# RWKV-7 scan of a diffusion trunk: each chunk as one affine map of the state, and triangular inverses begun on GpSimd with 16x16 blocks

## The chip, the cores and the metric

The kernel runs on one core of one Trainium2 chip. The metric is the time of one execution on the device in microseconds (us). A core has TensorE (PE in the profile, its weight loads PEld), VectorE (DVE), ScalarE (ACT), GpSimd (POOL) and SyncE (SP), which here only issues DMAs.

## The reference, cut to what matters

The program is a trunk of two layers over 512 latent tokens and 256 context tokens of width 1024. A layer is half a SwiGLU, a token mixer, and half a SwiGLU. The mixer of layer 0 is HGRN2, that of layer 1 is a bidirectional RWKV-7; the change lies in the scan of the latter. For each of 16 heads (64 wide) and each direction it computes, token by token,

```python
def step(s, inp):                       # s: 64 x 64 state of a head
    dec, kt, vt, kkt, bt = inp[:5]
    sa = jnp.einsum('bhvk,bhk->bhv', s, kkt)
    s = s * dec[:, :, None, :] - sa[..., None] * bt[:, :, None, :] + vt[..., None] * kt[:, :, None, :]
    y = jnp.einsum('bhvk,bhk->bhv', s, inp[5]) if with_out else None
    return s, y
```

first over the 256 context tokens, from a zero state and without outputs, then from that state over the 512 latent tokens.

## The kernel before

`rwkv_scan` works in chunks of 64 tokens. Within a chunk the 64 rank-one corrections depend on one another through a strictly triangular 64x64 matrix N, so a chunk needs the inverse of (I - N). With it the chunk is a few 64x64 products.

The work is cut into twelve items `(qd, g)`: `qd` is a group of four heads (0 to 3), `g` is 0 for the context and 1 or 2 for the two halves of the latent tokens. An item has two directions `d`, two head pairs `e`, two heads `hp` of a pair (on partitions 0 to 63 and 64 to 127) and four chunks `c`: 32 chunks of one head and direction. Five generators make an item:

- `prep_a` (line 1225) loads the features, forms the decays (`sw`, `cum`) and the scaled keys (`KR`, `BK`), multiplies them (`A`, line 1304), masks the products to N and Ar, and writes the 32x32 diagonal blocks of N to DRAM (`md`, line 1318) by eight DMAs on SP, one block to a partition: 64 blocks.
- `prep_m` (line 1323) is GpSimd's: it loads the blocks to 64 partitions (`M<-md`, line 1330), inverts each by 30 steps of two instructions (a product into `mt`, line 1336, an addition into `M`, line 1337) on up to 240 elements of a partition, and stores them (`me<-M`, line 1340).
- `prep_d` (line 1344) loads the inverted blocks into `P1` by eight DMAs on SP (`P<-me`).
- `prep_b` (line 1352) loads the values (`VU`), turns `BK` (`bkt`), and forms `W`, the part of the correction that the values alone give.
- `prep_c` (line 1386) transposes the blocks on VectorE (`PT`, line 1391) and forms the off-diagonal 32x32 blocks by 64 products of 32x32 (`TT`, line 1409, `Yo`, line 1411), copied into the inverse by four instructions.

`scan` (line 1430) then goes through four chunk steps one after another, for both directions and pairs at once, with the state in `G`. A step is four groups of products with work on other engines between them: `kG` (16 products), `rhs` = kG + W on VectorE, `U` = inverse times rhs (16), two copies of U into `VU` on ScalarE, `G` (16), two VectorE instructions that add the old state and scale it, and for latent items `y` (32 products, four of one kind and four of the other in turn) with two copies. `readout` normalizes a finished `qd`.

The main loop at line 1555 takes the items in order. While `scan` of item k yields, it advances the inversions (`RM` steps at each yield), the preparation of later items (`RP`: two steps of `prep_a` of k+2, then `prep_d` of k+1, the rest of `prep_a` of k+2, `prep_b` and `prep_c` of k+1), and the readout (`RO`). The tile framework takes this order and priorities (`urgent`), simulates a timeline, and fixes one order of instructions for each engine; on the chip every engine keeps its order and waits on semaphores. Buffers come in rings: `Q` of 13 and 15 tiles (`NQ1`, `NQ2`), PSUM banks of tag "a" (two, for `prep_a`), "b" (two, for `prep_b`, `prep_c` and the readout), "s" (four, for the scan).

Before the loop the value projection (`value_steps`) runs on PE beside the preparation and inversion of item 0. After it come the output projection and the last SwiGLU.

Of the kernel before, what the change touches and what calls it, by code (L numbers as in the profile page):

```python
# [9 lines left out]
F32 = mybir.dt.float32  # L10
# [16 lines left out]
NQ1, NQ2 = 13, 15  # L27
RM, RP, RO, RV, RF = 3.0, 5.0, 0.3, 1.5, 1.3
# [40 lines left out]
NCST = 790  # L69
# [4 lines left out]
def trunk(ctx, tc, io, phases=None, dump=None):  # L74
# [1105 lines left out]

    def rwkv_scan(l):
# [5 lines left out]
        masks = [cst2[:, 260 + 128 * d:388 + 128 * d] for d in range(2)]  # L1187
        PP = open_psum("PP")
# [3 lines left out]
        def Q(name):  # L1192
            first = "B2" not in late or name in Q1
            return (B1 if first else late["B2"]).tile([128, 1024], F32, tag="Q", name=name, bufs=NQ1 if first else NQ2)
# [18 lines left out]
        diagonal = [[B1.tile([128, 16, 64], F32, name=f"P1_{i}{d}") for d in range(2)] for i in range(2)]  # L1213
        for d in range(2):
            dve.memset(diagonal[0][d], 0.0)
            pool.memset(diagonal[1][d], 0.0)
        FE, ME = dve, pool
        slot = lambda hp, e, c: hp * 8 + e * 4 + c
# [3 lines left out]
        lanes = [(d, hp, b, d * 32 + (hp * 2 + b) * 8, 64 * hp + 32 * b) for d in range(2) for hp in range(2) for b in range(2)]  # L1222
        ready, inverse = {}, {}

        def prep_a(qd, g):
# [9 lines left out]
            gs = B1.tile([128, 4], F32, tag="gs", name="gs", bufs=3)  # L1235
# [84 lines left out]
            ready[qd, g] = KR, BK, N, Ar, gt, gs, md  # L1320
            yield

        def prep_m(qd, g):
# [4 lines left out]
            me = dram.tile([64, 32, 32], F32, tag="me", name="me", bufs=2)  # L1328
            M = Q("M")[0:64, :1024].rearrange("l (s t) -> l s t", t=32)
            pool.dma_start(out=M, in_=md)  # L1330
            eng = ME
            mt = B1.tile([64, 256], F32, tag="mt", name="mt", bufs=2)
            for j in range(30, 0, -1):
                n = 31 - j
                t = mt[:, :j * n].rearrange("l (a b) -> l a b", b=n)
                eng.tensor_tensor(t, M[:, 0:j, j:j + 1].to_broadcast([64, j, n]), M[:, j:j + 1, j + 1:32].to_broadcast([64, j, n]), ALU.mult)  # L1336
                eng.tensor_tensor(M[:, 0:j, j + 1:32], M[:, 0:j, j + 1:32], t, ALU.add)  # L1337
                yield
            eng.memset(M.rearrange("l s t -> l (s t)")[:, 0:1024:33], 1.0)
# [4 lines left out]
        def prep_d(qd, g):  # L1344
            while (qd, g) not in inverse:
                yield
            me = inverse[qd, g]
            P1 = inverse[qd, g] = diagonal[(3 * qd + g) % 2]
            for d, hp, b, l0, r0 in lanes:
                nc.sync.dma_start(out=P1[d][r0:r0 + 32, 8 * hp:8 * hp + 8, 32 * b:32 * b + 32], in_=me[l0:l0 + 8].rearrange("l s t -> s l t"))  # L1350

        def prep_b(qd, g):
            KR, BK, N, Ar, gt, gs, _ = ready[qd, g]
# [17 lines left out]
            W = Q("W").rearrange("p (i n) -> p i n", i=4)  # L1371
            for i2 in range(2):
                p = bank("W")
                for i in range(2):
                    for d in range(2):
                        c = chunk(d, 2 * i2 + i)
                        for e in range(2):
                            for hp in range(2):
                                o = 256 * i + 64 * (2 * d + e)
                                pe.matmul(p[half(hp), o:o + 64], N[d][half(1 - hp), slot(hp, e, c)],  # L1380
                                          VU[half(1 - hp), d, c, hp, e], start=True, stop=True)
                act.activation(W[:, 2 * i2:2 * i2 + 2], p.rearrange("p (i n) -> p i n", i=2), AF.Copy)
                yield
            ready[qd, g] = KR, N, Ar, BKT, VU, W, gt, gs

        def prep_c(qd, g):
            KR, N, Ar, BKT, VU, W, gt, gs = ready[qd, g]
            P1 = inverse.pop((qd, g))
            PT = [late["B2"].tile([128, 16, 32], F32, tag="PT0", name="PT0", bufs=1), Q("PT").rearrange("p (s n) -> p s n", n=64)]
            for d in range(2):  # L1390
                dve.transpose(PT[d], P1[d][:, :, :32 + 32 * d])
                yield
            Y = [P1[0], PT[1]]
# [3 lines left out]
            for stage in range(2):  # L1397
                for e in range(2):
                    for c in range(4):
                        for d in range(2):  # L1400
                            for hp in range(2):
                                s = slot(hp, e, c)
                                lo = 32 * (s % 8)
                                a = 64 * hp + 32 * d
                                b = 64 * hp + 32 * (1 - d)
                                ca, cb_ = 32 * d, 32 * (1 - d)
                                if stage == 0:
                                    other = (PT[0] if d == 0 else P1[1])[a:a + 32, s, ca:ca + 32]
                                    pe.matmul(pt[b:b + 32, lo:lo + 32], N[d][a:a + 32, s, cb_:cb_ + 32], other, start=True, stop=True, tile_position=(a, b))
                                else:  # L1410
                                    pe.matmul(py[a:a + 32, lo:lo + 32], tt[b:b + 32, lo:lo + 32], Y[d][b:b + 32, s, cb_:cb_ + 32], start=True, stop=True, tile_position=(b, a))
                    yield
                if stage == 0:
                    act.activation(tt, pt[:, :256], AF.Copy)
            for d in range(2):
                for hp in range(2):
                    a = 64 * hp + 32 * d
                    src = py[a:a + 32, :256].rearrange("p (s n) -> p s n", n=32)
                    dst = Y[d][a:a + 32, 8 * hp:8 * hp + 8, 32 * (1 - d):32 * (1 - d) + 32]
# [4 lines left out]
            ready[qd, g] = (KR, Ar, BKT, VU, Y, W, gt, gs)  # L1424
# [5 lines left out]
        def scan(qd, g, KR, Ar, BKT, VU, Y, W, gt, gs):  # L1430
# [4 lines left out]
            Gt = lambda: late["B2"].tile([128, 4, 64], F32, tag="G", name="G", bufs=3)  # L1435
            G = None
            if lat:
                G = Gt()
                dve.tensor_tensor(G, state["G"], gs.unsqueeze(2).to_broadcast([128, 4, 64]), ALU.mult)
            for i in range(4):  # L1440
                cs = (i, 3 - i)
                at = lambda d, e: slice(64 * (2 * d + e), 64 * (2 * d + e) + 64)
                if G is not None:
                    p = bank("kG", "s")
                    for d, e in DE:
                        for hp in range(2):
                            pe.matmul(p[half(hp), at(d, e)], KR[d][half(hp), 4 * e + cs[d], 0], G[half(hp), 2 * d + e], start=True, stop=True)
                    rhs = late["B2"].tile([128, 256], F32, tag="rhs", name="rhs", bufs=2)
                    dve.tensor_tensor(rhs, p[:, :256], W[:, i], ALU.add)
# [312 lines left out]
```

## Time and profile before

| | us |
|---|---|
| median of 3 runs | 3897.82 |
| lowest and highest of them | 3892.38 and 3904.64 |
| the profiled execution | 3901.05 |
| its span, first to last instruction | 3899.3 |
| mean granted TensorE clock, share of full | 0.926 |

An execution's time is its span plus about 2 us. The page of the profile gives for each engine the sum of the times of its instructions; matmuls are pipelined, so that the time of one is longer than the distance to the next. [...]

### The profile page before, as it was taken

The numbers are of one execution on the slowest core, as the hardware profiler recorded it, in microseconds if no ns is written. First come the engines' busy times: TensorE is split into PE (matmuls) and PEld (weight loads), VectorE is DVE, ScalarE is ACT, GpSimd is POOL, SyncE is SP. The second block draws the span as 40 slices with busy tenths as digits, with TensorE's granted clock in tenths as the row PEclk, the third lists the DMA queues.
The fourth block names the chain that finished last, engine by engine and source line by source line (L and its number), as shares of the span: only waits on it lengthen the run. The fifth ranks groups of instructions, "written<-read, shape, count | busy, mean of one in ns | idle before, by whom it ended". The sixth has DMA issues, their size and how long they took to land. (4 is left out here: it accounts for less than half of the span.)

```text
span 3899.3 us, 61645 instructions
## 1 busy us (share of the span) xinstructions
PE 3551.6 (91%) x24898; PEld 3115.9 (80%) x24898; DVE 2529.3 (65%) x4042; ACT 1310.4 (34%) x2024; POOL 1382.0 (35%) x1395
## 2 busy tenths in 40 slices
PE   5999998899999899999899999698978889889998
PEld 3898997688888688888799998576867777668887
DVE  6766667656666866666766675776444554468886
ACT  4332333232322432333532333354322222244343
POOL 4212213433433422122422221522366766523332
PEclk9999999999999899999999999798967776779999
DMA  5332331411112233333132332247633332233332
GB/s 186 115 96 88 97 98 44 114 43 44 39 44 66 66 113 103 103 110 113 52 95 82 90 95 78 66 155 240 164 88 81 83 82 63 61 106 91 94 93 81
DMA packets 517051, 362.52 MB, mean 93 GB/s; under 512 B 83517, under 2 KB 490333, under 8 KB 516766
## 3 DMA queue, kind: packets, MB, share of 16 engines
q1 hardware_dynamic: 513694, 350.19, 30.5%
q0 software_dynamic: 1920, 6.29, 0.7%
q8 instruction: 196, 3.21, 0.3%
q10 hardware_dynamic: 1152, 2.10, 0.2%
q14 instruction: 89, 0.73, 0.1%
HBM read 315.64 MB, written 42.87 MB: 92 GB/s over the span
## 5 line engine op out<-in xcount | busy, mean ns | idle before, releaser
L607 PE MATMUL po<-g,whi 128*128 128x512 f32 (+1 forms) x2464 | 593.4, 350 | 10.2 <-ACT g L211 10.2
L551 POOL TENSOR_TENSOR raw<-raw 128x512 f32<-128x512 f32 x88 | 124.9, 1419 | 1341.3 <-DMA raw<-in_ffn_w_in 772.4
L534 PE MATMUL c<-u,whi 128*128 128x386 f32 (+1 forms) x2112 | 524.5, 332 | 48.1 <-DVE uu L565 15.9
L526 ACT ACTIVATE whi<-raw 128x1024 fp32r<-128x1024 f32 x352 | 332.5, 950 | 570.4 <-PE po L607 306.9
L607 PEld LDWEIGHTS po<-g,whi 128*128 128x128 f32 x2464 | 406.2, 190 | 84.6 <-issue 11.4
L527 DVE TENSOR_TENSOR wlo<-raw,whi 128x1024 fp32r<-128x1024 f32 x352 | 416.4, 1187 | 32.3 <-ACT whi L526 30.6
L534 PEld LDWEIGHTS c<-u,whi 128*128 128x128 f32 x2112 | 371.6, 191 | 76.2 <-ACT u L446 25.1
L534 PE MATMUL a<-u,whi 128*128 128x386 f32 (+1 forms) x1408 | 347.4, 331 | 23.6 <-DVE u L428 17.2
L607 PE MATMUL po<-g,wlo 128*128 128x512 f32 (+1 forms) x1232 | 367.1, 348 | 0.0
L611 DVE SCALAR_TENSOR_TENSOR h<-po,mod,h 128x512 f32<-128x512 f32 (+1 forms) x384 | 228.3, 628 | 194.3 <-PE po L607 194.2
L534 PE MATMUL b<-u,whi 128*128 128x386 f32 (+1 forms) x1408 | 344.1, 329 | 2.3 <-ACT pp L562 1.4
L534 PE MATMUL c<-u,wlo 128*128 128x386 f32 (+1 forms) x1056 | 344.9, 327 | 0.0
L534 PEld LDWEIGHTS a<-u,whi 128*128 128x128 f32 x1408 | 251.8, 192 | 29.0 <-issue 18.4
L196 ACT ACTIVATE whi<-raw 128x1024 fp32r<-128x1024 f32 (+1 forms) x193 | 184.7, 959 | 266.8 <-PE c L534 108.5
L534 PEld LDWEIGHTS b<-u,whi 128*128 128x128 f32 x1408 | 246.5, 189 | 12.3 <-issue 6.6
L197 POOL TENSOR_TENSOR wlo<-raw,whi 128x1024 fp32r<-128x1024 f32 x48 | 127.0, 2647 | 302.7 <-ACT whi L196 284.1
L534 PE MATMUL a<-u,wlo 128*128 128x386 f32 (+1 forms) x704 | 233.1, 331 | 0.5 <-DVE wlo L527 0.5
L607 PEld LDWEIGHTS po<-g,wlo 128*128 128x128 f32 x1232 | 208.0, 190 | 29.8
L534 PE MATMUL b<-u,wlo 128*128 128x386 f32 (+1 forms) x704 | 229.2, 326 | 1.0 <-DVE wlo L527 1.0
L1336 POOL TENSOR_TENSOR mt<-M 64x168 f32<-64x168 f32 (+5 forms) x360 | 191.7, 533 | 67.6 <-DMA M<-md 41.2
L1337 POOL TENSOR_TENSOR M<-M,mt 64x168 f32<-64x168 f32 (+5 forms) x360 | 199.6, 555 | 26.4
L534 PEld LDWEIGHTS c<-u,wlo 128*128 128x128 f32 x1056 | 203.5, 193 | 0.0
(362 smaller groups left out, 7295.2 us busy)
## 6 DMA issues: line engine op xcount, KB each, us to landing
raw<-in_ffn_w_in SPq DMA_DIRECT2D x176, 512.0 KB
raw<-in_mod_w SPq DMA_DIRECT2D x144, 512.0 KB
raw<-in_ffn_w_out SPq DMA_DIRECT2D x80, 384.0 KB
raw<-in_hgrn_w_in SPq DMA_DIRECT2D x40, 512.0 KB
raw<-in_ffn_w_out SPq DMA_DIRECT2D x28, 512.0 KB
raw<-in_w_rkv SPq DMA_DIRECT2D x24, 512.0 KB
ld<-s_bk SPq DMA_DIRECT2D x48, 256.0 KB
s_bk<-knb SPq DMA_DIRECT2D x32, 192.0 KB
```

Of the source, the lines that this page charges most:

```text
L196: act.activation(hi[:, :m], raw[:, :m], AF.Copy)
L197: slots["lo"].tensor_tensor(lo[:, :m], raw[:, :m], hi[:, :m].bitcast(F32), ALU.subtract)
L526: act.activation(hi, x, AF.Copy)
L527: dve.tensor_tensor(lo, x, hi.bitcast(F32), ALU.subtract)
L534: pe.matmul(p[:, :q], a[:, c], x[k][:, b], start=first and k == 0 and i == 0, stop=k == 3 and i == 2, skip_group_check=not first)
L551: pool.tensor_tensor(S[:, lo], U[:, lo], U[:, hi], ALU.add)
L607: pe.matmul(p[v][:, :t1 - t0], wx[:, k, at:at + 128], x[:, e, t0:t1], start=k == 0 and i == 0, stop=k == nk - 1 and i == 2)
L611: dve.scalar_tensor_tensor(h[d][:, t0:t1], p[v][:, :t1 - t0], mods[l, sub, 2][:, d, v:v + 1], h[d][:, t0:t1], ALU.mult, ALU.add)
L1336: eng.tensor_tensor(t, M[:, 0:j, j:j + 1].to_broadcast([64, j, n]), M[:, j:j + 1, j + 1:32].to_broadcast([64, j, n]), ALU.mult)
L1337: eng.tensor_tensor(M[:, 0:j, j + 1:32], M[:, 0:j, j + 1:32], t, ALU.add)
```

## The change

Each 64-token chunk is turned ahead of the scan into an affine map of the state. With Y the inverse, `prep_b` also transposes the keys by a product with the identity (`kT`) and keeps them beside `W` in a tile `KW`; `prep_c` multiplies both by Y (`YK`, 128 columns at once), which gives the final `VU` and the keys' part; and a second group of products (`P`) folds that into `KR`: its first half becomes the identity plus the chunk's correction of the state, its second half the whole map from the state to the outputs. A step of `scan` is then one accumulated group of 32 products, one VectorE instruction for the new state, and, for every two steps, one group of 64 products for `y`: the 32 of one kind, then the 32 of the other. `kG`, `rhs`, `U`, the copies of U and the addition of the old state leave the scan.

GpSimd inverts 128 blocks of 16x16 on 128 partitions, by 14 steps of two instructions on up to 56 elements. The 32x32 level is made on TensorE from there: two groups of 64 products of 32x32 (`T16`, `R16`) with a mask, an addition, transposes and copies; the 64x64 level stays as `TT` and `Yo`. The blocks are moved by 16 DMAs of half the bytes instead of eight, at `md` and at `X`. Tile `N` has a ring of its own; the rates of the loop and sizes of rings are other ones.

```diff
-NQ1, NQ2 = 13, 15
-RM, RP, RO, RV, RF = 3.0, 5.0, 0.3, 1.5, 1.3
+NQ1, NQ2, NG = 13, 10, 5
+RM, RP, RO, RV, RF = 3.5, 9.0, 0.6, 1.5, 1.3
...
-            md = dram.tile([64, 32, 32], F32, tag="md", name="md", bufs=2)
+            md = dram.tile([128, 16, 16], F32, tag="md", name="md", bufs=2)
             for d, hp, b, l0, r0 in lanes:
                 nc.sync.dma_start(out=md[l0:l0 + 8].rearrange("l s t -> s l t"),
-                                  in_=(N[0] if d == 0 else NT_)[r0:r0 + 32, 8 * hp:8 * hp + 8, 32 * b:32 * b + 32])
+                                  in_=(N[0] if d == 0 else NT_)[r0:r0 + 16, 8 * hp:8 * hp + 8, 16 * b:16 * b + 16])
...
-            for j in range(30, 0, -1):
-                n = 31 - j
+            for j in range(14, 0, -1):
+                n = 15 - j
                 t = mt[:, :j * n].rearrange("l (a b) -> l a b", b=n)
...
-            W = Q("W").rearrange("p (i n) -> p i n", i=4)
...
+            for d in range(2):
+                ps_ = [bank(n).rearrange("p (e c n) -> p e c n", e=2, c=4) for n in ("kT", "W")]
+                for e in range(2):
+                    for c in range(4):
+                        for hp in range(2):
+                            pe.matmul(ps_[0][half(hp), e, c], KR[d][half(hp), 4 * e + c, 0], ident[half(hp), half(hp)], start=True, stop=True)
+                        for hp in range(2):
+                            pe.matmul(ps_[1][half(hp), e, c], N[d][half(1 - hp), slot(hp, e, c)], VU[half(1 - hp), d, c, hp, e], start=True, stop=True)
+                for x in range(2):
+                    act.activation(KW[d][:, :, :, x], ps_[x], AF.Copy)
...
+            p = view(bank("T16"))
+            for d in range(2):
+                for c in range(8):
+                    for hp, b, a in rows32:
+                        pe.matmul(p[a:a + 32, d, c], N[d][a:a + 32, 8 * hp + c, 32 * b:32 * b + 32], X[a:a + 32, 1, d, c], start=True, stop=True, tile_position=(a, a))
+                yield
+            dve.tensor_tensor(t16.rearrange("p d s n -> p (d s) n"), p.rearrange("p d s n -> p (d s) n"), off16.unsqueeze(1).to_broadcast([128, 16, 32]), ALU.mult)
...
+            dve.tensor_tensor(flat(A), flat(X[:, 0]), flat(p), ALU.add)
+            dve.transpose(flat(AT), flat(A))
+            for hp, b, a in rows32:
+                act.activation(Y[a:a + 32, :, :, 32 * b:32 * b + 32], A[a:a + 32], AF.Copy)
...
+            for d in range(2):
+                for e in range(2):
+                    p = bank("YK")
+                    pv = p.rearrange("p (c x n) -> p c x n", c=4, x=2)
+                    for c in range(4):
+                        for hp in range(2):
+                            pe.matmul(p[half(hp), 128 * c:128 * c + 128], Y[half(hp), d, 4 * e + c], KW[d][half(hp), e, c].rearrange("p x n -> p (x n)"), start=True, stop=True)
+                    act.activation(KW[d][:, e, :, 0], pv[:, :, 0], AF.Copy)
+                    for hp in range(2):
+                        if hp:
+                            dve.tensor_copy(VU[half(hp), d, :, hp, e], pv[half(hp), :, 1])
+                        else:
+                            act.activation(VU[half(hp), d, :, hp, e], pv[half(hp), :, 1], AF.Copy)
...
+                    kr = KR[d][:, 4 * e:4 * e + 4]
+                    dve.tensor_tensor(kr[:, :, 0], pv[:, :, 0], unit.unsqueeze(1).to_broadcast([128, 4, 64]), ALU.add)
+                    if lat:
+                        dve.tensor_tensor(kr[:, :, 1], pv[:, :, 1], kr[:, :, 1], ALU.add)
...
-                if G is not None:
-                    p = bank("kG", "s")
...
-                    dve.tensor_tensor(rhs, p[:, :256], W[:, i], ALU.add)
...
+                    if G is not None:
+                        for n, (d, e) in enumerate(DE):
+                            for hp in range(2):
+                                pe.matmul(p[half(hp), at(d, e)], KR[d][half(hp), 4 * e + cs[d], 0], G[half(hp), 2 * d + e], start=False, stop=True, skip_group_check=True)
+                    G = late["B2"].tile([128, 4, 64], F32, tag="G", name="G", bufs=NG)
+                    dve.tensor_tensor(G, p[:, :256].rearrange("p (s n) -> p s n", n=64), gt[:, :, i].unsqueeze(2).to_broadcast([128, 4, 64]), ALU.mult)
```

## Rows read from the trace of the kernel before

**Rows 1.** The scan, 2820 to 3430: PE, PEld, DVE, ACT, POOL busy; clock; DMA share; GB/s.

```profile
2820.00:3430.00 610.00, 516.01 (x6918) 434.11 (x6916) 282.95 (x641) 147.07 (x354) 368.10 (x693) 0.72 0.31 78
```

**Rows 2.** Chain of waits, 3030 to 3140: start, length, what.

```profile
3033.92 4.12 DMA M<-md
...
3075.91 3.19 DMA me<-M
3079.99 1.75 DMA P<-me
3081.84 0.71 DVE PT L1391
...
3088.41 3.10 DMA M<-md
```

**Rows 3.** Waits in the scan: total us, times, longest.

```profile
DVE PT L1391 <- DMA P<-me: 80.5, 13, 12.7
```

**Rows 4.** Waits of PE in the scan.

```profile
PE TT L1409 <- DVE PT L1391: 24.1, 4, 13.5
PE U L1456 <- DVE rhs L1449: 12.2, 10, 4.2
...
PE kG L1447 <- DVE G L1472: 10.3, 3, 6.4
```

**Rows 5.** GpSimd by form in the scan: busy us, mean ns, idle before.

```profile
L1337 POOL TENSOR_TENSOR M<-M,mt 64x240 f32<-64x240 f32 x22 | 16.5, 750 | 1.7
...
L1337 POOL TENSOR_TENSOR M<-M,mt 64x58 f32<-64x58 f32 x22 | 7.3, 332 | 0.8
```

**Rows 6.** SP's issues, 3076 to 3092: start, length.

```profile
3079.12 3.78 SPq L1350 DMA_DIRECT2D P<-me  x8
```

**Rows 7.** PE in order of time, 3180 to 3246: start, length, products.

```profile
3185.00 0.69 PE L1466 MATMUL G<-VU,BKT 128*64 128x64 f32 x16
3185.62 1.16 PE L1304 MATMUL A<-KR,BK 64*128 64x128 f32 x8
...
3213.88 0.48 PE L1484 MATMUL y<-KR,G 64*64 64x64 f32 x4
3214.29 0.48 PE L1482 MATMUL y<-Ar,VU 128*64 128x64 f32 x4
...
3235.19 1.12 PE L1447 MATMUL kG<-G,KR 64*64 64x64 f32 x16
3236.24 3.35 PE L295 MATMUL bkt<-cst,BK 128*128 128x128 f32 x14
```

**Rows 8.** PE in order of time, 3366 to 3390.

```profile
3368.05 0.34 PE L1482 MATMUL y<-Ar,VU 128*64 128x64 f32 x4
3368.32 0.33 PE L1484 MATMUL y<-KR,G 64*64 64x64 f32 x4
...
3371.48 1.03 PE L1380 MATMUL W<-VU,N 64*64 64x64 f32 x29
```

**Rows 9.** Chain of waits, 2700 to 3450: a group of 32x32 products.

```profile
3003.51 1.00 PE Yo L1411 x64
```

**Rows 10.** Short stretches: columns as in rows 1.

```profile
2890.60:2894.00 3.40, 0.00 (x0) 0.00 (x0) 0.87 (x2) 0.00 (x0) 3.40 (x12) 0.62 0.28 86
...
3154.30:3157.70 3.40, 3.40 (x57) 2.79 (x58) 0.42 (x1) 0.38 (x1) 3.01 (x6) 0.50 0.03 5
...
3390.40:3393.80 3.40, 2.41 (x76) 2.06 (x76) 2.35 (x4) 0.22 (x1) 0.00 (x0) 0.50 0.83 223
```

**Rows 11.** DVE by line in the scan: busy us, mean ns, idle before.

```profile
L1310 DVE TENSOR_TENSOR N<-A,cst 128x256 f32<-128x256 f32 x88 | 36.0, 418 | 52.2 <-PE A L1304 49.7 <-POOL M L1337 2.1
...
L1391 DVE STREAM_TRANSPOSE PT<-P 128x512 f32<-128x512 f32 (+1 forms) x24 | 23.4, 975 | 85.5 <-DMA P<-me 85.5
...
L1471 DVE TENSOR_TENSOR G<-G 128x256 f32<-128x256 f32 x40 | 16.7, 416 | 43.7 <-PE G L1466 43.6
```

**Rows 12.** ACT by line in the scan.

```profile
L1460 ACT ACTIVATE VU<-U 64x256 f32<-64x256 f32 x96 | 36.3, 378 | 128.1 <-PE U L1456 126.5
```

More of the change, by code (lines that the diff above doesn't have):

```diff
@@ L1369, in prep_b @@
                     yield
-            W = Q("W").rearrange("p (i n) -> p i n", i=4)
[L1372 to L1382, printed above, removed]
+            KW = [Q("KW").rearrange("p (e c x n) -> p e c x n", e=2, c=4, x=2) for _ in range(2)]
@@ new lines, in prep_c @@
+            p = view(bank("R16"))
+            for d in range(2):
+                for c in range(8):
+                    for hp, b, a in rows32:
+                        pe.matmul(p[a:a + 32, d, c], t16[a:a + 32, d, c], X[a:a + 32, 0, d, c], start=True, stop=True, tile_position=(a, a))
+                yield
+            A, AT = tile_of("A32"), tile_of("AT32")
+            dve.tensor_tensor(flat(A), flat(X[:, 0]), flat(p), ALU.add)
+            dve.transpose(flat(AT), flat(A))
+            for hp, b, a in rows32:
+                act.activation(Y[a:a + 32, :, :, 32 * b:32 * b + 32], A[a:a + 32], AF.Copy)
@@ L1434, in scan @@
             yb = state.get("y")
[L1435 to L1439, printed above, removed]
+            G = state["G"] if lat else None
+            at = lambda d, e: slice(64 * (2 * d + e), 64 * (2 * d + e) + 64)
+            if g < 2:
+                dve.tensor_tensor(gt[:, :, 3], gt[:, :, 3], decays[qd, g + 1], ALU.mult)
@@ L1440, in scan @@
+            Gs = []
             for i in range(4):
                 cs = (i, 3 - i)
-                at = lambda d, e: slice(64 * (2 * d + e), 64 * (2 * d + e) + 64)
-                if G is not None:
-                    p = bank("kG", "s")
[L1445 to L1448, printed above, removed]
-                    dve.tensor_tensor(rhs, p[:, :256], W[:, i], ALU.add)
-                    yield
-                else:
-                    rhs = W[:, i]
@@ L1453, in scan @@
-                p = bank("U", "s")
-                for d, e in DE:
-                    for hp in range(2):
-                        pe.matmul(p[half(hp), at(d, e)], Y[d][half(hp), slot(hp, e, cs[d])], rhs[half(hp), at(d, e)], start=True, stop=True)
-                for hp in range(2):
-                    v = VU[half(hp), 0, i, hp].rearrange("p e n -> p (e n)")
-                    dst = bass.AP(v.tensor, v.offset, [list(v.ap[0]), [1024 + 256 * (3 - 2 * i), 2], [1, 128]])
-                    act.activation(dst, p[half(hp), :256].rearrange("p (d n) -> p d n", d=2), AF.Copy)
@@ L1491, in scan @@
                         else:
[L1492 removed]
+                            dve.tensor_tensor(dst, dst, pv[:, :, d], ALU.add)
                     yield
[L1494 removed]
             state["G"] = G
```

151 lines of the change are left out of this document (85 added, 66 removed).

## Prediction

> **What bounds the kernel now.** I first asked the view by stretches where the changed generators run. They run from 2820 us, where the value projection has ended, to 3430 us, where the last `y` product is copied: 610 us of the 3899 us span [rows 1]. The other 3289 us execute the same instructions before and after, so I forecast no change there. Within the 610 us the reader should see three numbers: PE is busy 516.0 us (85%), GpSimd 368.1 us (60%), and the granted clock is 0.72. Twelve items in 610 us make 50.8 us an item.
>
> Neither share is near 100%, so the next view is the chain of waits [rows 2]. One round reads: the blocks of an item land for GpSimd from 3033.92 on (4.12 us); GpSimd computes until it stores them at 3075.91 (37.9 us); the store takes 3.19 us; the eight loads end at 3081.7; VectorE transposes (0.71 us); and only at 3088.41 does the next item's load of blocks start. The last gap exists because VectorE keeps its order: the transposition stands in its queue ahead of work of the next item's `prep_a`, which N and so `md` need. The round is 54.5 us, close to the 50.8 us of an item. The waits agree: VectorE stands 80.5 us of the stage waiting for those loads [rows 3], and PE 24.1 us behind that transposition [rows 4]. So GpSimd's chain sets the pace. But it does so with PE 85% busy at a low clock. What PE needs when GpSimd's part is short therefore decides the result, more than GpSimd's saving.
>
> **GpSimd's part.** Removed: 60 instructions an item on up to 240 elements, of which the largest takes 750 ns here [rows 5]. In their place are 28 on at most 56 elements; the nearest row is 332 ns at 58 [rows 5]. With the 0.08 us that lies between two instructions in the row's idle time (1.7 us for 22) I take 28 x 0.41 = 11.5 us an item instead of 37.9. No row has this form on 128 partitions; I take them to cost what 64 do, and if they cost twice that it would be 23 us, still far under 38.
>
> **DMAs on SP.** `md` and `X` take 16 issues each instead of eight. Eight took 3.78 us [rows 6], 0.47 each, so both add 7.6 us of SP's time to an item, and each load is finished about 3.8 us later. The chain from `md` to `X` becomes about 4.1 + 11.5 + 3.2 + 7.6 + 1.8 = 28 us [rows 2, 6]. It starts where `prep_a` of item k+2 ends and is needed by `prep_c` of that item, about one item later. I hide it under the 40-odd us of PE's work of an item; if it were not hidden, 28 us is still less than the 50 us it replaces. Queued behind the later `X` loads on SP are the next loads of keys and values, which are asked for several us ahead.
>
> **PE's part, in work at the full clock.** PE's busy time times the granted clock is 516.0 x 0.72 = 372 us of full-clock work [rows 1]. To this come, per item, at full-clock prices:
> - `kT`: 64 products of 64x64 at the price of `W`, 1.03 us for 29, 0.0355 each [rows 8]: +2.3 us.
> - `T16` and `R16`: 128 products of 32x32; 64 took 1.00 us [rows 9], 0.0156 each: +2.0 us.
> - `YK`: 32 products of 128 columns. None like them is in the trace. Bounds are 0.0355 (64 columns on a quarter of the array [rows 8]) and 0.145 (128 columns on half of it, 1.16 us for 8 [rows 7]). I take 0.07, twice the first, since they use a quarter of the array with twice the columns: +2.2 us (1.1 to 4.6).
> - `P`: 64 products (32 for a context item) at the price of `G`, 0.62 us from start to start for 16, 0.039 [rows 7]: +2.5 (1.25).
> - `U` gone: 64 x 0.039 = -2.5.
> - `kG` changes only its place; it becomes the second half of `G`.
> - `y`: the four-and-four alternation costs 0.27 us for 4, 0.0675 each [rows 8]; sixteen of one kind cost 0.039 [rows 7]. At the half clock it is 0.41 for 4, 0.1025, against 1.05 for 16, 0.066 [rows 7]. So the alternation itself has a price of about 0.028. The new order, 16 and 16, loses it: -128 x 0.028 = -3.6 for the eight latent items. If the price were that of the operands, this term would be 0.
>
> The sum is +2.9 for a latent item and +5.25 for a context item: 8 x 2.9 + 4 x 5.25 = +44 us, so 416 us of work; with the bounds of `YK` and `y`, 403 to 474. PE gets more work from the change, not less.
>
> [...]
>
> **What clock.** The clock falls behind each pause: it is 0.62 in a stretch where PE does nothing while GpSimd works, and 0.50 behind the last such pause [rows 10]. It also falls without one: PE is busy all of the stretch at 3154 at 0.50, on small products. I counted 20 falls in the stage; 7 lie behind the wait for a transposition, of which rows 10 show the first and the last. At 0.72 the clock is at its half level for 56% of the time. If those 7 falls go and the cold time shrinks with them, 56% x 13/20 = 36% stay cold: 0.82. PE's busy time becomes 416/0.82 = 507 us.
>
> **Idle time of PE.** Now 610 - 516 = 94 us. The wait behind the transposition goes (-24), so do those of `U` on `rhs` and of `kG` on G (-12 and -10) [rows 4]; the new step still waits for its own VectorE instruction once, for which I put back 12. That leaves 60.
>
> **The other engines.** VectorE gains 8 evictions of 256 columns in `P`, 4 in `YK`, and `T16` and A of 512, at 0.418 per 256 [rows 11]: 16 x 0.418 = 6.7; transposes of about the same size as those that go (1.95 an item [rows 11]); and it loses `rhs`, the addition of the state (0.416 each [rows 11], about seven an item) and some small ones, -3.5. With +3.2 an item it goes from 283 to 321 us of some 570: not a bound. ScalarE loses the copies of U (36.3 us [rows 12]) and gains fourteen copies an item, six of 512 columns and eight of 256; at 0.378 per 256 [rows 12] that is 91 us: 147 becomes about 200.
>
> **Sum.** The stage becomes 507 + 60 = 567 us instead of 610: -43 us. The first item's preparation and the last one's scan lie open in both, the one longer, the other shorter; I take nothing. The profiled execution, 3901.05 us, would become 3858; it lies 3 us over the median of the runs, so I predict **3855 us**. A measurement here tells about 0.3% (12 us) from no change.
>
> **Rivals.**
> 1. *The clock comes up nearly fully*, since PE is never starved any longer. At 0.95: 416/0.95 = 438, with 50 idle 488: -122, 3776 us. For it: behind pauses the clock is low. Against it: the fall at 3154 had no pause, and `T16` and `R16` add just such small products. Chance 0.18.
> 2. *The clock stays and PE is the bound: slower.* At 0.72, 416 us of work take 578 us; with 60 idle 638: +28, 3926 us. It decides from a clock of 416/550 = 0.756 downwards. For it: more and smaller products, PE already at 85%. Against it: seven of twenty falls lose their cause. With clocks near 0.756 the result is within 0.3%. Chance 0.13 for slower, 0.14 for the same.
> 3. *PSUM banks.* `prep_b`, `prep_c` and the readout share two banks, and an item fills 20 instead of 8. If each of the 12 added fills stops PE for 0.6 us of an eviction (between one of 0.378 and two of 0.418 [rows 11, 12]), that is 86 us more idle time: 653, +43, 3941 us; it decides from 0.3 us a fill. For it: the copies of one bank must follow one another. Against it: products of the scan and of `prep_a` have other banks. Chance 0.07. [...]
> 4. *GpSimd still sets the pace*, its chain only shorter: 28 us an item is below PE's 45, so this can't last; counted with the first.
>
> **Numbers.** The forecast case has 0.48, its own range 3815 to 3885 us (work 403 to 440, clock 0.80 to 0.85). Faster: 0.48 + 0.18 = 0.66; same 0.14; slower 0.20. The range reaches from 3765, near the first rival, to 3930, which takes in the second.
>
> **What would show it.** Right: GpSimd's instructions under 0.4 us and its busy time in the stage under 160 us; VectorE hardly waiting for `X`; PE over 88% busy in a stage of 540 to 590 us, clock 0.79 to 0.86; `y` products at 0.04 at the full clock. Wrong: a clock at 0.75 or below, PE waiting for copies out of `YK`, `P` or `T16`, or `prep_a` of a later item held back by a ring, which the present trace doesn't price.

## The result and the profile after

The changed kernel takes 4037.06 us (median; 4029.55 to 4039.15) against 3895.6 us of the kernel before beside it: ratio 1.0356, 95% interval 1.0333 to 1.0379, **slower**, where 3855 was forecast. The profiled execution has a span of 4033.6 us. Ahead of 2820 us the two traces agree (PE is busy 2615.4 and 2616.1 us), and behind the last scan they differ by 5.6 us; the stage itself, from 2820 us to the last `y` addition, takes 739.6 us instead of 610.9. By stretches (columns as in [rows 1]):

```profile
2820.00:3559.60 739.60, 550.06 (x11964) 484.82 (x11964) 265.62 (x689) 180.45 (x410) 96.03 (x341) 0.78 0.21 53
```

PE is busy 550 us (516 before) and idle 190 us (94 before); GpSimd falls from 368 to 96. So the part that was to become short did, and most of what was lost is waiting. The waits of that stage (engine, line, tile, what it waited for: us, times, longest):

```profile
POOL M L1342 <- DMA hw_s<-s_hw: 292.6, 6, 57.7
POOL M L1342 <- DMA md<-NT: 241.0, 5, 56.2
DVE X L1404 <- DMA X<-me: 155.3, 21, 16.1
ACT Y L1429 <- DVE A L1426: 126.0, 12, 18.1
...
PE TT L1442 <- DVE AT L1427: 83.5, 12, 13.4
```

GpSimd now waits 534 us for work: it is no longer the bound. But VectorE stands 155.3 us before the transposition of X (80.5 in [rows 3], 85.5 over the whole stage in [rows 11], for the one it replaces), and PE 83.5 us for `AT`, which VectorE makes behind it (24.1 in [rows 4]). One round shows why. SP's issues, then GpSimd's, then VectorE's, in order of time (start, length, ..., idle time before and what ended it):

```profile
3141.29 3.87 SPq L1330 DMA_DIRECT2D md<-NT  x8
...
3163.18 7.43 SPq L1363 DMA_DIRECT2D X<-me  x16
...
3207.67 4.59 SPq L1330 DMA_DIRECT2D md<-NT  x8
```

```profile
3148.64 0.54 POOL L1342 DMA_DIRECT2D M<-md  x1 [56.76 <-DMA hw_s<-s_hw]
...
3161.13 0.59 POOL L1352 DMA_DIRECT2D me<-M  x1 [0.30 <-POOL M L1349]
```

```profile
3153.35 0.69 DVE L1418 TENSOR_TENSOR t<-T,cst 128x512 f32<-128x512 f32 x1 [3.37 <-PE T L1416]
3168.25 0.45 DVE L1404 STREAM_TRANSPOSE X<-X 128x256 f32<-128x256 f32 x1 [14.21 <-DMA X<-me]
3168.62 0.65 DVE L1426 TENSOR_TENSOR A<-X,R 128x512 f32<-128x512 f32 x1
...
3173.42 0.45 DVE L1404 STREAM_TRANSPOSE X<-X 128x256 f32<-128x256 f32 x1 [3.40 <-DMA X<-me]
```

The chain `md`, GpSimd, `me`, X takes 3141.29 to 3168.25 = 27 us, to the second transposition 32. That is the 28 us of the prediction. But the transposition waited for at 3168 is that of the *next* item, and it stands on VectorE ahead of work of the *current* one: of the eleven items that have a next one, between `t` and `A` in five, between `A` and `AT` in one, behind `AT` in five, and in all of them its first half stands ahead of the copies into Y. So `YK`, `P` and the scan of an item, and in six items `TT` too, wait for the blocks of the item after it. The masks that make N stand behind it as well, so the first eight issues of the next `md` come at 3177.79 and the last eight, which GpSimd needs too, at 3207.67: the round is 3141.29 to 3207.67, 66 us.

### The profile page after: what moved, and what is told of

It reads as the page before. It is cut to its first block, busy times and chain, and to the rows that moved or that the text cites. A ratio compares the mean times of both kernels' runs of the same rounds, so it can differ in the third digit from the quotient of the medians.

```text
span 4033.6 us, 71753 instructions
## 1 busy us (share of the span) xinstructions
PE 3585.8 (89%) x29954; PEld 3166.9 (79%) x29954; DVE 2513.4 (62%) x4108; ACT 1346.0 (33%) x2080; POOL 1083.1 (27%) x1011
## 4 chain that ended last, share of the span: by engine, by line
PE 36%; DVE 6%; DMA 3%; SPq 2%; POOL 2%; issue 2%; ACT 1%; DVEq 0%; POOLq 0%; ACTq 0%
PE po L607 8%; PE c L534 5%; PE a L534 4%; PE b L534 3%; PE v L222 2%; PE YK L1467 2%; SPq L1363 2%; PE k L222 2%; PE A L1316 1%; POOL mt L1348 1%; PE G L1514 1%; POOL M L1349 1%; PE P L1481 1%; DMA M<-md 1%; DVE wlo L527 1%
## 5 line engine op out<-in xcount | busy, mean ns | idle before, releaser
L607 PEld LDWEIGHTS po<-g,whi 128*128 128x128 f32 x2464 | 406.2, 190 | 84.6 <-issue 11.4
L197 DVE TENSOR_TENSOR wlo<-raw,whi 128x768 fp32r<-128x768 f32 (+1 forms) x145 | 176.2, 1217 | 37.1 <-ACT whi L196 36.8
```

Source lines behind the costliest of these rows:

```text
L197: slots["lo"].tensor_tensor(lo[:, :m], raw[:, :m], hi[:, :m].bitcast(F32), ALU.subtract)
L607: pe.matmul(p[v][:, :t1 - t0], wx[:, k, at:at + 128], x[:, e, t0:t1], start=k == 0 and i == 0, stop=k == nk - 1 and i == 2)
```

## Experiments

Times are medians; each ratio is against runs of the kernel before on the same chip. e2b_fixed leaves the inverses out of the result and the two e12 runs a part of them: they show what these cost, and are no kernels to use. "Stage" runs from 2820 us to the last `y` addition of the profiled execution; idle is the stage less PE's busy time.

| run | us | ratio (95%) | stage | PE busy | idle | clock |
|---|---|---|---|---|---|---|
| before | 3895.6 | 1 | 610.9 | 516.6 | 94 | 0.72 |
| after | 4037.06 | 1.0356 (1.0333 to 1.0379) | 739.6 | 550.1 | 190 | 0.78 |
| e1_order | 3926.43 | 1.0066 (1.0049 to 1.0084) | 629.4 | 548.6 | 81 | 0.84 |
| e3_splitq | 4029.3 | 1.0333 (1.0318 to 1.0349) | 737.7 | 555.7 | 182 | 0.79 |
| e7_rates | 4109.81 | 1.0538 (1.052 to 1.0556) | 819.0 | 629.4 | 190 | 0.78 |
| e2b_fixed | 3941.26 | 1.0108 (1.0091 to 1.0125) | 638.4 | 541.1 | 97 | 0.84 |
| e8_twice | 4004.09 | 1.0265 (1.025 to 1.028) | 706.1 | 581.7 | 124 | 0.81 |
| e12b_no16 | 3859.33 | 0.9909 (0.989 to 0.9927) | 559.4 | 488.8 | 71 | 0.88 |
| e9_y | 3900.09 | 1.0002 (0.9992 to 1.0011) | 609.2 | 459.2 | 150 | 0.74 |
| e5_half16 | 3920.92 | 1.005 (1.0033 to 1.0066) | 635.5 | 564.5 | 71 | 0.76 |
| e5n_newrates | 3944.91 | 1.012 (1.0103 to 1.0137) | 651.4 | 512.9 | 139 | 0.75 |
| e10_early | 3888.94 | 0.9973 (0.9963 to 0.9983) | 602.7 | 456.0 | 147 | 0.74 |
| e11_early | 3916.4 | 1.0036 (1.0022 to 1.005) | 629.4 | 511.6 | 118 | 0.72 |

**The order on VectorE** (e1_order). The transpositions get a tile of their own with one buffer, and a one-column addition that reads it and the last `P` copy holds the next item's transpositions behind them. (`A` is written into the tile of `t`, by two additions instead of one.)

```diff
-dve.transpose(X[:, 1 - d, d]...., X[:, d, d]....)
+XT = late["B2"].tile([128, 2, 8, 32], F32, tag="XT", name="XT", bufs=1)
+dve.transpose(XT[:, d]...., X[:, d, d]....)
...
+dve.tensor_tensor(last[:, 0:1], XT[:, 0, 0, 0:1], KR[1][:, 7, 0, 0:1], ALU.add)
```

> The changed kernel with one thing moved: the transposes of an item's 16x16 blocks write a tile of their own that is free only when the keys of the item before are folded (a one-column addition behind the last P copy reads it), so on VectorE they can't stand before the additions and copies of the item before. Theory A (in VectorE's fixed order the transposes of the next item stand ahead of the A, Y and VU instructions of this one, so the chain md, GpSimd, me, X of some 30 us lies in line in every round): VectorE's wait for X falls from 166 us to under 80, PE's idle time in the scan stage from 190 us to about 110, time 3930 to 3980 us. Rival B (the added products and the two PSUM banks make the stage long): no change, 4020 to 4045. Rival C (the chain is a loop of its own through the rings and would be in line in any order): no change, 4020 to 4045, with the wait moved behind the other instructions.

3926.43 us, 110.6 less than the changed kernel and a little under the range of theory A; it is still 0.66% above the kernel before. VectorE no longer waits for X (3.8 us before these transpositions in the whole stage, for another transfer); PE's wait for `AT` falls from 83.5 to 20.6 us, PE idles 81 us instead of 190 and the granted clock rises from 0.78 to 0.84, with the same busy time:

```profile
2820.00:3449.40 629.40, 548.62 (x11965) 483.82 (x11964) 270.97 (x715) 180.43 (x410) 97.73 (x341) 0.84 0.26 63
```

The chain has not become shorter: in one round of e1_order `md` starts at 3148.88 and the last load of X ends at 3181.67, 33 us (29 in the round of the changed kernel above). SP, then VectorE, which finds the blocks there:

```profile
3148.88 4.90 SPq L1331 DMA_DIRECT2D md<-NT  x8
3172.92 8.75 SPq L1364 DMA_DIRECT2D X<-me  x16
```

```profile
3184.91 0.16 DVE L1494 TENSOR_TENSOR last<-XT,KR 128x1 f32<-128x1 f32 x1
3185.32 0.84 DVE L1406 STREAM_TRANSPOSE XT<-X 128x256 f32<-128x256 f32 x2 [0.24 <-DVE last L1494]
```

**What arrives late** (e2b_fixed: the blocks for X come from a constant array, the inverses are left out; e3_splitq: eight of the sixteen loads are issued by GpSimd; e7_rates: the rates of before in the changed kernel).

```diff
-in_=me[l0:l0 + 8].rearrange("l s t -> s l t"))      # e2b_fixed
+in_=fixed[l0:l0 + 8].rearrange("l s t -> s l t"))
-nc.sync.dma_start(out=X[...                         # e3_splitq
+(nc.sync if d == 0 else pool).dma_start(out=X[...
-RM, RP, RO, RV, RF = 3.5, 9.0, 0.6, 1.5, 1.3        # e7_rates
+RM, RP, RO, RV, RF = 3.0, 5.0, 0.3, 1.5, 1.3
```

> The changed kernel with one thing other: the 16x16 blocks that go into X come from a constant array of identity blocks in DRAM, so X waits for no inversion (GpSimd still computes and stores its blocks, and nothing reads them: the inverses are left out of the result). Theory A (VectorE meets the transposition of X ahead of the current item's work, and X is late because the chain from md to X is long): the wait of VectorE for X goes from 155 us to under 30, and the time falls to about the version with the order guard, 3900 to 3945 us. Rival B (the added work of PE and its banks would hold the stage at its length whatever X does): the time stays above 4000 us. Rival C (the 16 loads of X themselves, on SP's queue, are late, not what they carry): VectorE keeps 60 us or more of that wait and the time lies between 3950 and 4010 us.

> The changed kernel with eight of the 16 X loads of an item issued by GpSimd, whose queue is empty then, beside eight on SP. The last X lands about 3.5 us earlier. Theory A and rival C: the chain is in line in each of twelve rounds, so 30 to 45 us off: 3990 to 4010. Rival B: within 10 us of 4037.

> The changed kernel with the rates of the loop as they were (3.0, 5.0, 0.3 in place of 3.5, 9.0, 0.6). The preparation is then spread wider over the shorter scans and the rest of it follows in a lump behind each scan. Theory A: the place of the transposes in VectorE's order hardly depends on the rates, 4000 to 4070. If the rates are the cause: under 3980.

With constant blocks 96 us go: the wait for X is 45.7 us (theory A said under 30) and the time 3941. So the loads alone are not what is late. But this run does not leave VectorE's order alone: the framework fixes the order from the arrival that it simulates, and with blocks that are always there it put the transpositions an item further ahead (two pairs lie before the stage, one in the changed kernel) and behind `A` wherever the two meet. It moves arrival and order together; e1_order is the run that moves the order alone. Splitting the loads gave 8 us, less than expected, and the intervals of the two ratios overlap: the transposition that blocks is the first one, and its eight loads stand first on SP in either kernel (3.65 us for them, 7.43 for all sixteen). The old rates cost 73 us more, which I did not expect; PE is then busy 629 us with the same products, and the wait for X is no longer (142.6 us). The traces hold a likely reason. The rows give each product a form, such as `128*64` or `64*64`. Taken in PE's order, with sizes rounded up to 32, 64 or 128, the form changes 706 times in the stage of e7_rates and 467 times in that of the changed kernel: 239 more changes and 79 us more busy time, 0.33 us a change. The same count gives 664 for the kernel before and 422 for e9_y below (57 us, 0.24 a change), and 782 for e5_half16 and 576 for e5n_newrates (52 us, 0.25). For the rates this is a reading of the traces; only e9_y changes the alternation on purpose.

**The 32x32 products** (e8_twice: T16 and R16 issued twice; e12b_no16: both left out, with their mask, addition and banks). Both stand on the version with the order guard.

```diff
-                for c in range(8):                    # e8_twice, T16 and R16
+                for c in [*range(8), *range(8)]:
-            t16 = tile_of("t16")                      # e12b_no16
...
+            dve.tensor_copy(XT[:, 2], X[:, 0, 0])
...
+            upper, lower = [XT[:, 0], X[:, 1, 1]], [XT[:, 2], XT[:, 1]]
...
+            A, AT = lower, upper
```

> The version with the order guard, and the two groups of 32x32 products, T16 and R16, issued twice (the second pass writes the same values). A product of f32 leaves two records in the trace, so this adds 256 instructions an item, 3072 in all. Theory D (the prediction counted one record a product and so took half of the real price; a 32x32 record costs 0.0156 us at either clock): +4.0 us of busy time an item, 48 us in all; with PE setting the pace the time rises by 35 to 60 us over the version with the guard (3926), to 3961 to 3986. Rival E (the count of the prediction was right, and what the version with the guard has over the forecast is waiting): +2.0 us an item, 24 us in all at the most, to 3935 to 3950 us, and PE's busy time in the stage rises by 25 us, not by 48.

> The version with the order guard (3926.4 us) without the groups T16 and R16, their mask, their addition and their two banks: the 32x32 blocks between the 16x16 ones are left out of the inverse. Doubling the two groups cost 78 us, 46 of it busy time and the rest pauses of PE between those small products. Theory Q (the pauses belong to the small products, so the two groups cost as much where they stand first): 60 to 85 us less, 3841 to 3866 us. Rival R (the pauses come from the doubled length alone, and the first pass costs only its busy time of 46 us, part of it hidden): 25 to 46 us less, 3880 to 3901 us. If Q holds, the affine maps themselves cost no more than the 610 us stage of before.

> The version with the order guard without T16 and R16 (the 32x32 blocks between the 16x16 ones are left out of the inverse), with one more VectorE copy so that ScalarE's copies into Y stand behind the guard too. Theory Q (the pauses of PE belong to the small products, so the two groups cost as much in the first place as their doubling, 78 us): ScalarE and VectorE wait less than 20 us for X and the time is 3841 to 3866 us, below the kernel before. Rival R (only the busy time counts, and the affine maps are what is dear): 3880 to 3901 us.

Doubling costs 77.7 us, more than either theory gave; leaving out gains 67.1, in the range of theory Q. Groups of e1_order, then of e8_twice (instructions, busy us, mean ns, idle before):

```profile
L1426 PE MATMUL R<-XT,t 32*32 32x32 f32 x768 | 12.7, 215 | 9.6 <-issue 9.6
L1419 PE MATMUL T<-X,N 32*32 32x32 f32 x768 | 12.7, 194 | 4.5 <-issue 4.4
L1426 PE MATMUL R<-X,t 32*32 32x32 f32 x768 | 11.3, 207 | 15.1 <-DVE t L1421 9.7 <-issue 5.5
...
L1419 PE MATMUL T<-XT,N 32*32 32x32 f32 x768 | 9.7, 194 | 5.6 <-ACT KW L1395 4.9 <-issue 0.7
```

```profile
L1426 PE MATMUL R<-XT,t 32*32 32x32 f32 x1536 | 25.7, 234 | 21.4 <-issue 21.4
L1426 PE MATMUL R<-X,t 32*32 32x32 f32 x1536 | 25.4, 233 | 21.3 <-issue 11.2 <-DVE t L1421 10.1
L1419 PE MATMUL T<-X,N 32*32 32x32 f32 x1536 | 24.1, 210 | 27.0 <-issue 27.0
...
L1419 PE MATMUL T<-XT,N 32*32 32x32 f32 x1536 | 17.5, 194 | 11.3 <-issue 6.2 <-ACT KW L1395 4.9
```

The busy time doubles, 46.4 to 92.7; and the pauses put down to "issue", in which PE waits for nothing that the profile shows, grow from 20.2 to 65.8 us. PE in order of time, e8_twice, one item:

```profile
3192.26 0.84 PE L1419 MATMUL T<-XT,N 32*32 32x32 f32 x75 [0.61 <-ACT KW L1395]
3193.69 0.66 PE L1419 MATMUL T<-XT,N 32*32 32x32 f32 x53 [0.59 <-issue]
3194.20 0.90 PE L1419 MATMUL T<-X,N 32*32 32x32 f32 x74
3197.37 0.97 PE L1419 MATMUL T<-X,N 32*32 32x32 f32 x54 [2.26 <-issue]
3199.22 1.24 PE L1426 MATMUL R<-X,t 32*32 32x32 f32 x74 [0.88 <-DVE t L1421]
3201.36 0.91 PE L1426 MATMUL R<-X,t 32*32 32x32 f32 x51 [0.90 <-issue]
...
3205.39 0.96 PE L1426 MATMUL R<-XT,t 32*32 32x32 f32 x54 [2.10 <-issue]
```

A product of f32 is two such instructions (the 64 products of `T`, issued twice, leave the 256 above). A burst runs at 0.84/75 = 0.011 us each at 3192.26 and at 1.24/74 = 0.017 at 3199.22. In the trace of the changed kernel 73 of `R` take 0.81 us where the granted clock is 1.00 (3220.41), 0.011 each, and 82 of `R` take 1.33 us where it is 0.50 (3033.38), 0.016. The 0.0156 of [rows 9], which the expectation takes for both clocks, was measured at 0.50, as the stretch of that group in the trace of before shows (PE alone; clock, DMA share, GB/s):

```profile
3003.65:3004.50 0.85, 0.85 (x66) 0.50 0.00 0
```

But in e8_twice a pause of 0.6 to 2.3 us comes every 127 or 128 instructions, so the 256 of `T` take from 3192.26 to 3198.34, 0.024 each, and those of `R` 7.13 us, 0.028.

The first try without the two groups (e12_no16, 3943.93 us, ratio 1.0127) is the old fault on another engine: ScalarE's copies into Y now read X straight from the DMA, stood ahead of the current item's copies, and waited:

```profile
ACT Y L1417 <- DMA X<-me: 132.9, 37, 14.7
```

One VectorE copy that puts them behind the guard is the difference to e12b_no16: 84.6 us. Theory Q's other sign did not come: VectorE waits 25.7 us for X there, and ScalarE 129 us for `XT`, where under 20 was expected. Of the stage's 70 us, 60 are busy time (46.4 of the two groups, the rest with the clock, 0.88 instead of 0.84) and only 10 idle time, though the pauses of the groups made 20: PE now waits 40 us for G on VectorE (4.9 in e1_order). So the 67 us are shown, and how they divide between pauses and busy time is not.

**The kernel before: y alone, and the turned order** (e9_y: only the pairing of `y`; e10_early: that, and all of `prep_a` of k+2 ahead of the loads of P of k+1; e11_early: the order without the pairing). The pairing needs five buffers of G instead of three, so one of the 15 tiles of `Q` goes.

```diff
-                if lat:                               # e9_y, e10_early
+                if lat and i % 2:
...
-SEQ = 'Adabc'                                         # e10_early, e11_early
+SEQ = 'Aadbc'
+dve.tensor_tensor(last[:, d:d + 1], P1[d][:, 0, 0:1], turns[3 * qd + g + 1][:, 0, 0:1], ALU.add)
```

> The kernel before with one part of the change alone: y is computed for two chunks at once, sixteen products of one kind and then sixteen of the other, instead of four and four. Theory I (the alternation has a price of its own, 0.028 us a record, 29 us of PE's work in all, and GpSimd's chain still sets the pace of the stage): y costs 1.08 us for 32 at the full clock, PE is busy 20 to 40 us less in the stage, and the time falls by no more than 15 us: 3880 to 3905 us. Rival J (PE's work sets the pace of before too): the time falls by 25 us or more, under 3878 us. Rival K (the later y holds up the readout): slower by more than 10 us.

> The kernel before with y for two chunks at once, and the order turned the way that GpSimd's chain needs: the inversions stay in 32x32 blocks on GpSimd, the loop takes all of prep_a of item k+2 ahead of the loads of P of item k+1, and a one-column VectorE addition that reads P and the NT of item k+2 holds those loads and the transpositions of PT behind it on both queues, so that md of item k+2 no longer waits for me of item k+1. Theory L (the stage of before is paced by the round md, GpSimd, me, P, PT, next md, of 54.5 us, and PE's work is not its bound): the round shrinks to GpSimd's own 37.9 + 4.1 + 3.2 us = 45 to 48, VectorE's wait for P goes from 80 us to under 30, PE's idle time in the stage falls below 110 us, and the time comes out between 3830 and 3875 us, below both kernels. Rival M (the clock or ready waits of PE set the pace, GpSimd's round only fills it): 3885 to 3905 us. Rival N (P now comes too late for the item's own scan): slower than 3910 us, with PE waiting for PT.

> The same turned order on the kernel before, but with y left four and four. Theory L: PE has some 50 us more to do in the stage than in the run with y for two chunks, and with the round at 46 us an item (550 us in all) PE is the bound: 15 to 40 us slower than that run, 3860 to 3895. Rival M: the same time as that run within 8 us, as y alone changed nothing on the kernel before.

Pairing takes 57 us of busy time from PE (516.6 to 459.2) and nothing from the time: PE's work does not pace the kernel before; PE waits instead, and VectorE's wait for P grows from 85.5 to 103.5 us. In the turned order the same pairing is worth 27 us (3916.4 to 3888.9), inside theory L's 15 to 40. But the rest of L did not come: 3889 instead of 3830 to 3875, the wait for P 106 us where under 30 was expected, and the turned order alone is 0.36% slower. e10_early is the only version with the whole result that is below both kernels; its 0.27% is clear of its interval, but too small to call it faster.

**Other mixtures** (e5_half16: 16x16 blocks, order guard, scan of before, old rates; e5n_newrates: the same at the new rates; e13_affine32: affine maps with the 32x32 inversions on GpSimd; e13b_affine32: with ScalarE's copies behind the guard; e14_affine32_early: with the turned order). The three e13 and e14 runs advance the inversions at twice the rate (RM 7.0), and the rings of `Q` differ by a tile.

```diff
-RM, RP, RO, RV, RF = 3.0, 5.0, 0.3, 1.5, 1.3          # e5n_newrates against e5_half16
+RM, RP, RO, RV, RF = 3.5, 9.0, 0.6, 1.5, 1.3
-md = dram.tile([128, 16, 16], F32, tag="md", ...)     # e13_affine32, e13b, e14
+md = dram.tile([64, 32, 32], F32, tag="md", ...)
```

> The order guard, the 16x16 blocks on GpSimd with T16 and R16 on PE, and y for two chunks at once, but the scan of before (kG, rhs, U, G) in place of the affine maps, at the rates of before: kT, YK and P are left out. By the corrected count its work of PE at the full clock is 372 + 12 x 8.0 (T16 and R16, 512 records an item at 0.0156) - 8 x 3.6 (y) = 439 us against 488 for the whole change. Theory F (with the wait for X gone the stage is PE's work over the clock plus some 80 us of idle time): 439/0.84 + 80 = 603 us, 7 less than before: 3880 to 3905 us. Rival G (the scan's longer chain of four links a chunk, no longer covered by anything, sets the pace): PE idles 110 us or more in the stage, 3920 us or more. Rival H (the clock rises above 0.88 with fewer small products of YK and P): under 3870 us.

> The version with 16x16 blocks, the order guard and the scan of before (3920.9 us at the old rates), with the rates of the changed kernel (3.5, 9.0, 0.6). With the whole change the old rates cost 73 us more, but there the preparation is twice as long. Theory O (the rates only decide how soon prep_b and prep_c of the next item are issued, and what held this version was the low clock of 0.76 behind finer interleaving): 3885 to 3915 us and a clock of 0.79 or more. Rival P (the clock is set by the kind of products, and the rates do nothing): 3915 to 3930 us, clock 0.76.

> A version with the affine maps and the order guard, but with the inverses begun as before, with 32x32 blocks on GpSimd (60 instructions an item, eight DMAs each way, inversions advanced at twice the rate); T16 and R16 are not needed. Theory S (with the order guard md of the next items no longer waits for X, so GpSimd's 45 us an item lie beside PE's some 45): the time comes within 15 us of the version without T16 and R16, 3845 to 3885 us, below both kernels. Rival T (GpSimd's chain of 28 + 26 us, about 54 us from md to X, is longer than an item and sets the pace): VectorE or PE waits 60 us or more for X, 3890 to 3940 us.

> The affine maps with the 32x32 inversions of before on GpSimd, the order guard, and ScalarE's copies into Y behind the guard too. Theory S (GpSimd's 45 us an item lie beside PE's 45): within 20 us of the version without T16 and R16, and below the kernel before. Rival T (the chain from md over GpSimd to X takes 54 us, starts only when prep_a of that item ends, and its loads of X stand ahead of the next md on SP, so it sets the pace): VectorE waits 60 us or more for X, 3900 to 3960 us.

> The same with all of prep_a of item k+2 ahead of the loads of X of item k+1, which are held behind its NT by a one-column VectorE addition. Theory S and T both expect that it takes less than the run without it if the chain sets the pace there: by 20 us or more, 3850 to 3890 us. If the run without it is PE's own (S), it changes nothing or costs up to 20 us, as prep_b and prep_c then come later.

All miss their first theory: 3920.92, 3944.91, 4006.73 (ratio 1.0283), 4016.22 (1.0299) and 4044.02 (1.0372). With e5_half16 less work is done at a lower clock, 0.76 (its expectation counts 512 instructions of T16 and R16 an item, where the rows have 256); the new rates leave that clock, take 52 us of busy time and add 68 of waiting, so neither O nor P held. The affine maps on 32x32 blocks are paced by GpSimd's chain, as theory T has it, though beyond its 3900 to 3960 us: VectorE waits 205 us for X in e13b_affine32. SP, GpSimd and VectorE of e13b_affine32:

```profile
3074.82 3.97 SPq L1363 DMA_DIRECT2D X<-me  x8
3078.89 1.89 SPq L1331 DMA_DIRECT2D md<-NT  x4
...
3125.25 3.76 SPq L1363 DMA_DIRECT2D X<-me  x8
```

```profile
3082.58 0.52 POOL L1343 DMA_DIRECT2D M<-md  x1 [10.14 <-DMA md<-NT]
...
3122.32 0.59 POOL L1353 DMA_DIRECT2D me<-M  x1 [0.29 <-POOL M L1350]
```

```profile
3059.33 1.23 DVE L1328 STREAM_TRANSPOSE NT<-N 128x1024 f32<-128x1024 f32 x1
...
3128.69 0.45 DVE L1405 STREAM_TRANSPOSE XT<-X 128x256 f32<-128x256 f32 x1 [17.21 <-DMA X<-me]
```

NT is ready at 3060.6, but its `md` stands behind the loads of X on SP until 3078.89; then GpSimd takes 40 us, and VectorE waits 17 us. The turned order of e14_affine32_early was to mend that and cost 28 us more; why was not settled.

## Why the prediction was wrong

**The step that failed first: "I hide it under the 40-odd us of PE's work of an item"**, said of the chain from `md` to X. Its length was right (28 forecast, 27 to 32 measured), and so was the time at which X is needed: in e1_order the first `T` on these blocks starts 62 us behind their `md` (3210.56 and 3148.88), about one item. What I did not ask is where the instruction that *waits* for X stands. The prediction saw in [rows 2] that VectorE keeps its order and that a transposition holds up later work; it then let the wait vanish because the data would come sooner. The transposition came sooner too: it stands ahead of work of the current item, so nothing lies between to hide under. Shown by e1_order, which gives 110.6 us back with a chain that is no shorter; e2b_fixed (96 us back) agrees, but changes the order too. Rival 4, that GpSimd's chain still sets the pace, was put aside since 28 us is less than an item; the round of 66 us is that chain and the current item's own work in line, not beside each other.

**The second: the sum of PE's work, 416 us.** In its own unit, busy time times clock (a rough one: the mean clock of a stretch counts its idle time too, and four `y` took 0.41 us at a clock of 0.50 and 0.27 at 1.00 [rows 7, 8], 1.5 times as long and not twice), e1_order has 548.6 x 0.84 = 461. Between runs the terms separate: `y` 372 to 340 (e9_y, 459.2 x 0.74): -32, forecast -29, right. T16 and R16 461 less 430 (e12b_no16, 488.8 x 0.88): +31, forecast +24. The affine maps 430 less 340: +90, forecast `kT` 27.6 + `YK` 26.4 + `P` 25 - `U` 30 = +49. The cause is a count: the rows count two instructions for a product of f32, and for T16, R16, `YK` and `P` I multiplied products by the price of one instruction. The groups of the changed kernel show it (768 instructions of `YK` are 12 x 32 products, twice):

```profile
L1467 PE MATMUL YK<-KW,Y 64*64 64x128 f32 x768 | 69.9, 336 | 13.3 <-DVE Y L1457 13.3
...
L1481 PE MATMUL P<-BKT,KW 64*64 64x64 f32 x768 | 51.8, 234 | 0.1
...
L1484 PE MATMUL P<-Ar,KW 64*64 64x64 f32 x512 | 42.9, 239 | 0.0
```

With the right count the affine term is 27.6 + 53.8 + 50 - 30 = 101, nearer to 90. The price taken for `YK` was right: 32 took 2.01 us at a clock of 1.00 (from 2996.21 in the changed kernel), 0.063 against 0.07. For T16 and R16 the right count alone would give 48 instead of 24, too much; the other half of that error is their price.

**The third: the price of T16 and R16.** The sum is at the full clock, but [rows 9] is at 0.50. At the full clock a burst has 0.011 an instruction, and 12 x 256 x 0.011 = 34, near the +31 measured: half the count at too high a price came out near by luck. What the price leaves out is time and not work: 0.0156 came from 64 instructions in a row, the groups here have 128 and more, and a row that shows a burst does not show the pauses between bursts. The extra 3072 instructions of e8_twice cost 77.7/3072 = 0.025 us each, and the groups that stand there anyway cost 67 us (e12b_no16), where 24 of work at a clock of 0.82 are 29. In the trace of e8_twice that time is bursts, at 0.011 to 0.018 us an instruction, and the pauses between them, which grew by 45.6 us.

**Right.** GpSimd: 9.7 us from the landing of the blocks to the store (11.5 forecast), 96 us busy (under 160), 128 partitions at 56 elements 0.29 to 0.30 us. The clock: 0.82 forecast, 0.84 once the order is mended; 0.78 with the waits. In the trace of before it stands at 1.00 or at 0.50 and at nothing between, at 0.50 for 337 of the 610 us (55%, where the prediction has 56% from the mean). Of its 21 falls in the stage 14 come with a pause of PE of over 2 us, between the pause's start and 1.5 us behind its end, and seven without one. The falls were not counted again in the trace of the changed kernel, so the number agrees and its reason is not shown. ScalarE: about 200 forecast, 180. VectorE was put too high, 321 against 266. Idle time: 60 forecast, 81 in e1_order.

The 182 us between forecast and result are thus some 111 of order, 42 of busy time (549 less 507) and 21 of idle time (81 less 60), with 8 left over. Rival 2's mechanism, a clock that stays at 0.72, did not come. Rival 3, the banks, has no run of its own, but the rows speak against it: ahead of `P` PE idles 0.1 us in the whole stage, ahead of `YK` 13.3, and those for Y; only ahead of `T` are there some 5 us for copies out of `kT` and `W`, where the rival needed 86. The range of the forecast case does not follow from its own bounds either: 440 of work at a clock of 0.80 and 60 idle make 610 us, the stage of before, and so some 3898 and not 3885. And 3859.33 of e12b_no16, close to the 3855 forecast, confirms nothing: it lacks a part of the work.

## What to carry to other kernels

When a chain gets shorter, look where its consumer stands in its engine's order: VectorE waited 155.3 us for X with the transposition ahead of the current item's work, and not for it with the transposition behind that work (e1_order). What counts is how late the data is *for that place*, and an order fixed from an optimistic arrival put the wait ahead of work that needed nothing. Work saved on an engine that did not set the pace was worth nothing until the order let it (`y`: 0 us in one order, 27 in another). Count instructions, not products (768 for the 384 products of `YK`), and price small products from a stretch as long as the one to come, with the granted clock of that stretch beside it.

## What was not expected of the hardware

The run of 32x32 products of e8_twice above pauses every 127 or 128 matmul instructions, for 0.6 to 2.3 us, while the profile shows no wait. The spacing goes on across the groups: 53 and 74 instructions lie between two pauses, then 54 and 74, though PE waits for `t` in between. In the changed kernel, with 256 such instructions an item, the pauses last 0.5 to 2.4 us: four items have two of them, 127 or 128 instructions apart, seven have one, and the first has none. The profile counts a weight load to each matmul instruction (14997 and 14998 in the stage of e8_twice). No run here changes the spacing: what makes the pauses is not shown.
